# Sharing out the gate tiles anew among the convolution groups and the last head of attention

## The chip, the cores and the metric

The kernel runs on one core of a Trainium2 chip. TensorE (PE in the profile) does matrix products and transpositions, VectorE (DVE) and ScalarE (ACT) do the elementwise work, SyncE (SP) issues the transfers. The metric is the time of one execution in microseconds (us). All work is in fp32; PE takes it in the form fp32r, and each product is made of three (high by high, high by low, low by high part).

## What is computed

Two layers over 512 latent tokens and 256 context tokens with 1024 channels each. A layer does this, cut to what matters here:

```
proj = a @ w_in                        # a: modulated, normalised input
q, k, v -> differential attention of 4 heads
proj[P0:H0] -> pooling of 4 groups
proj[H0:G0] -> short convolution; z = x1 * longconv(v); y = x2 * longconv(z)
g = sigmoid(proj[:, G0:])              # 3 x 1024 gate columns
merged = g0 * attention + g1 * pooling + g2 * convolution
h = h + merged @ w_out ;  then a gated feed-forward layer
```

In layer 0 everything is done for latent and context tokens (768 columns), in layer 1 the context only gives keys and values, so that most products there have 512 columns.

## The kernel before

**Units.** A column tile of 128 outputs of `w_in` is a unit (`units`, L257 on): one load of 512 KB into `wr` (L268), the split into `wh` by ACT (L252) and `wl` by DVE (L253), 24 pairs of matmuls (layer 0: 512 and 256 columns each, 48 matmuls; layer 1: 24 of 512) into an accumulator tile `d` in PSUM (L285), and an eviction. There are two accumulators `d` in layer 0 and three in layer 1.

**Gate units.** 24 units for each layer give the gates (`gates`, `gate`). Their eviction is one sigmoid on ACT (L935) into a tile `gt`, and a store to DRAM (`gsp`, L936), from where the merge reads it back later. Nothing else waits for them.

**Convolution groups.** The 512 channels of the long convolution are taken in four groups of 128. A group begins with three units (`hyena_in`: v, x1, x2), whose eviction (`short`) is one ACT instruction (L895) and four of DVE (L899) in layer 0. Then come the steps of `stage`: F makes the filter's spectrum (L672 to L710), S transposes v and x1 (L839, L840) and transforms them, 1 is the spectral product on DVE (`spectral`, L791 to L795), M goes back and forward again (L863 on), 2 is the second product, Z the last transformation (L880, L881). The small letters f, s, q, m, w, z are the same steps for the context.

**The order.** `PROG` writes the order out by hand, one string for each layer; h is a unit of the next group, g takes the next gate unit off the list:

```
        if what == "g":
            gates.pop(0)()
            norm_more(2)
            return
...
            dense += units(win, 8, [12 + h], a, rng, pool)
            dense += qkv_units(h + 1) if h + 1 < HEADS else gates
```

The letters are priorities, no more: the framework's scheduler fixes each engine's order when the kernel is built, and lets an engine take a later letter's instruction where its own cost model says that the earlier one is not ready. On the chip each engine then works its list in order.

**Attention.** The first head's three units (v, k, q) follow the string's first part. Then for each of the four heads `HEAD` orders scores (L1053, L1054), exponentials (L1066, L1070), transpositions (L1094) and values (L1109); each f in it takes one unit off `dense` (`fill`): the head's pooling unit (`pool`) and the next head's three. The last head has no next head, and its list is the pooling unit and whatever is left of `gates`. Within attention the tile `gt` comes from the pool `pp` of five buffers, all of which one pooling unit uses.

Of the kernel before, what the change touches and what calls it, by code (L numbers as in the profile page):

```python
# [36 lines left out]
NCOL = 129  # L37
FFN_PARTS = ((6, 5, 5, 6), (8, 7, 7))

PROG = ('FggS1ggMfs2gggZgqmFwhhhSz1gMfs2ggZqmFwhhhSz1ggMfs2ggggZggqmFwhhhSz1gMfs2gggZgqm wz',  # L40
        'FgS1gggMFhhhS2ggZgg1gMFhhhS2ggZgg1ggMFhhh2ggSZg1ggggM 2gZ')
HEAD = ("01rfrA23fcrVfBrfU", "01rfrfrA23fVcfBrfU")


# [100 lines left out]
def build(ctx: ExitStack, tc: tile.TileContext, io: dict, out: bass.AP, dbg=None):  # L145
# [763 lines left out]
    def layer(l, a, hs, first, prepare):  # L909
# [73 lines left out]

        early, late = PROG[l].split()
        for what in early:
# [540 lines left out]
```

## Time and profile before

| | |
|---|---|
| median of 3 runs | 2394.58 us (2389.93 to 2403.16) |
| profiled execution, its own time | 2393.87 us |
| its span, first to last instruction | 2392.1 us |
| PE busy | 2325.6 us (97%) |
| DVE busy | 1722.3 us (72%) |
| ACT busy | 983.6 us (41%) |
| mean granted clock of PE | 0.991 |

Busy time is the union of an engine's instructions. The ends of matmuls are modelled, so PE counts as busy in stretches where it has little room as well as where it has none. The clock is a share of 2.4 GHz; it is granted at 1.00 or at 0.50 (1.2 GHz), and what stands between is a mean over the window.

### The profile page before, as it was taken

What the parts mean: (1) busy time and instruction counts of PE and PEld (TensorE: products, weight loads), DVE (VectorE), ACT (ScalarE), POOL (GpSimd) and SP (SyncE); (2) the same over time, 40 slices, a digit from 0 to 9 for tenths busy, and PEclk for the clock granted to TensorE, in tenths of its full rate; (3) what the DMA queues carried; (4) which work ended last, traced back from release to release, by engine and by line L of the source; (5) the groups of instructions that cost most, each with busy time, mean ns of one, the idle gap of its engine ahead of it and who ended that gap; (6) DMA issues with size and microseconds to landing.
All of it is one profiled execution on the core that took longest, in us unless ns stands there. A gap on an engine that the chain in (4) does not pass through costs nothing. (4 is left out here: it accounts for less than half of the span.)

```text
span 2392.1 us, 33306 instructions
## 1 busy us (share of the span) xinstructions
PE 2325.6 (97%) x12834; PEld 1981.7 (83%) x12834; DVE 1722.3 (72%) x3135; ACT 983.6 (41%) x1657; POOL 2.7 (0%) x8
## 2 busy tenths in 40 slices
PE   6999899999999999999999999999999999999998
PEld 3888688888878878888888888888888789888888
DVE  5688877999888785666768726899888778333336
ACT  6433334367762352121133424433377635312223
POOL 0000000000000000000000000000000000000000
PEclk9999899999989999999999999999999999999999
DMA  7222132321137543444725525344311444332324
GB/s 265 71 96 81 44 103 71 124 95 67 45 133 253 185 156 130 130 146 158 232 88 170 167 98 162 125 165 162 119 56 46 168 152 154 113 97 95 96 92 150
DMA packets 117801, 302.47 MB, mean 126 GB/s; under 512 B 13445, under 2 KB 27397, under 8 KB 116618
## 3 DMA queue, kind: packets, MB, share of 16 engines
q1 hardware_dynamic: 117642, 300.34, 37.9%
q8 instruction: 101, 1.65, 0.3%
q14 instruction: 58, 0.48, 0.1%
HBM read 266.74 MB, written 33.55 MB: 126 GB/s over the span
## 5 line engine op out<-in xcount | busy, mean ns | idle before, releaser
L252 ACT CAST wh<-wr 128x1024 fp32r<-128x1024 f32 (+3 forms) x327 | 331.0, 1013 | 933.2 <-PE d L285 756.1
L285 PE MATMUL d<-ah,wh 128*128 128x512 f32 (+1 forms) x2320 | 707.4, 354 | 6.8 <-ACT si L1371 2.8
L285 PE MATMUL d<-al,wh 128*128 128x512 f32 (+1 forms) x2320 | 709.9, 354 | 0.1
L285 PE MATMUL d<-ah,wl 128*128 128x512 f32 (+1 forms) x2320 | 706.6, 353 | 2.1 <-DVE wl L253 2.0
L253 DVE TENSOR_TENSOR wl<-wr,wh 128x1024 fp32r<-128x1024 f32 (+3 forms) x327 | 383.5, 1173 | 163.4 <-ACT wh L252 153.5
L285 PEld LDWEIGHTS d<-ah,wh 128*128 128x128 f32 x2320 | 387.8, 188 | 71.7 <-ACT si L1371 3.2
L285 PEld LDWEIGHTS d<-ah,wl 128*128 128x128 f32 x2320 | 388.8, 188 | 64.1 <-DVE wl L253 3.0
L285 PEld LDWEIGHTS d<-al,wh 128*128 128x128 f32 x2320 | 389.0, 188 | 61.5 <-DVE al L350 0.8
L489 DVE SCALAR_TENSOR_TENSOR junk<-mr,cb 128x512 bf16<-128x512 f32 x256 | 176.4, 689 | 13.4 <-DMA mr<-in_w_mod_rows_dram 8.2
L285 PE MATMUL d<-hh,wh 128*128 128x512 f32 (+1 forms) x584 | 179.1, 341 | 3.4 <-DVE h L1406 3.4
L285 PE MATMUL d<-hh,wl 128*128 128x512 f32 (+1 forms) x584 | 178.9, 341 | 0.0
L285 PE MATMUL d<-hl,wh 128*128 128x512 f32 (+1 forms) x584 | 178.7, 341 | 0.0
L1380 DVE TENSOR_TENSOR si<-d,si 128x512 f32<-128x512 f32 (+2 forms) x48 | 36.9, 768 | 174.3 <-PE d L285 174.3
L285 PE MATMUL d<-xs,wh 128*128 128x512 f32 x576 | 145.0, 358 | 0.8 <-ACT mx L1183 0.6
L1406 DVE SCALAR_TENSOR_TENSOR h<-d,mod,h 128x512 f32<-128x512 f32 (+1 forms) x96 | 58.5, 615 | 83.3 <-PE d L285 83.0
L285 PEld LDWEIGHTS d<-hh,wh 128*128 128x128 f32 x584 | 102.4, 190 | 17.9 <-issue 3.8
L285 PEld LDWEIGHTS d<-hl,wh 128*128 128x128 f32 x584 | 102.2, 190 | 13.6
L285 PEld LDWEIGHTS d<-hh,wl 128*128 128x128 f32 x584 | 102.4, 190 | 13.1
L285 PEld LDWEIGHTS d<-xs,wh 128*128 128x128 f32 x576 | 94.7, 189 | 18.1 <-ACT mx L1183 0.9
L285 PE MATMUL d<-xs,wl 128*128 128x512 f32 (+1 forms) x288 | 87.7, 358 | 0.0
L795 DVE TENSOR_TENSOR Y<-Y,T 128x1024 f32<-128x1024 f32 (+1 forms) x80 | 84.7, 1059 | 0.2
L794 DVE TENSOR_TENSOR T<-U,K 128x1024 f32<-128x1024 f32 (+1 forms) x80 | 83.1, 1059 | 0.0
(294 smaller groups left out, 3207.8 us busy)
## 6 DMA issues: line engine op xcount, KB each, us to landing
wr<-in_w_in_dram SPq DMA_DIRECT2D x104, 512.0 KB, 3.4
wr<-in_w_ffn_in_dram SPq DMA_DIRECT2D x96, 512.0 KB, 3.3
mr<-in_w_mod_rows_dram SPq DMA_DIRECT2D x160, 256.0 KB, 3.6
wr<-in_w_out_dram SPq DMA_DIRECT2D x32, 512.0 KB, 3.3
ksp<-K SPq DMA_DIRECT2D x28, 384.0 KB, 2.8
K<-ksp SPq DMA_DIRECT2D x8, 1344.0 KB, 7.7
wr<-in_w_ffn_out_dram SPq DMA_DIRECT2D x24, 448.0 KB, 3.4
gsp<-gt SPq DMA_DIRECT2D x24, 384.0 KB, 2.5
```

What stands on the lines that cost most here:

```text
L252: A.copy(hi, src)
L253: V.tensor_tensor(out=lo, in0=src, in1=hi.bitcast(F32), op=ALU.subtract)
L285: PE.matmul(o, w[:, c0:c0 + P], x[k][xi][:, c:c + nn], start=(k == 0 and pi == 0), stop=(k == K - 1 and pi == 2))
L489: V.scalar_tensor_tensor(out=junk[:], in0=raw[hf], scalar=1.0, in1=cb[v][hf][:, 0:512], op0=ALU.mult, op1=ALU.mult, accum_out=pv[:, v, hf, ...
L794: V.tensor_tensor(out=t[:], in0=ub, in1=kb, op=ALU.mult)
L795: V.tensor_tensor(out=y[:], in0=y[:], in1=t[:], op=ALU.add)
L1380: V.tensor_tensor(out=sg[f][:, cs], in0=o, in1=sg[f][:, cs], op=ALU.mult)
L1406: V.scalar_tensor_tensor(out=hs[d][:, cs], in0=o, scalar=mods[l][:, 40 + d, s:s + 1], in1=hs[d][:, cs], op0=ALU.mult, op1=ALU.add)
```

## The change

```diff
-PROG = ('FggS1ggMfs2gggZgqmFwhhhSz1gMfs2ggZqmFwhhhSz1ggMfs2ggggZggqmFwhhhSz1gMfs2gggZgqm wz',
-        'FgS1gggMFhhhS2ggZgg1gMFhhhS2ggZgg1ggMFhhh2ggSZg1ggggM 2gZ')
+PROG = ('FggS1gMfs2ggZgqmFwhhhSz1ggMfs2gggZqmFwhhhSz1ggMfs2ggZgqmFwhhhSz1gMfs2gggZgqm wz',
+        'FgS1gggMFhhhS2ggZgg1gMFhhhS2ggZgg1ggMFhhh2ggSZg1ggM 2gZ')
```

In layer 0 the four groups held 8, 3, 8 and 5 letters g and hold 6, 5, 5 and 5; 24 become 21, and the three gate units left over go to the last head of attention, which had none. In layer 1 the last group loses two of the four g between its first product and M; 23 become 21, and the last head gets three gate units in place of one. The number of units, their order in the list of gates and every instruction in them stay the same.

## Rows read from the trace of the kernel before

**Rows 1.** DMA issues of the page: a gate tile's store (KB, us to landing).

```profile
gsp<-gt SPq DMA_DIRECT2D x24, 384.0 KB, 2.5
```

**Rows 2.** Windows of 10 us: PE, PEld, DVE, ACT, POOL busy, clock, DMA share, GB/s.

```profile
250.00:260.00 10.00, 5.14 (x22) 4.31 (x21) 9.54 (x14) 3.25 (x5) 0.00 (x0) 0.83 0.17 52
260.00:270.00 10.00, 2.98 (x15) 2.16 (x14) 9.84 (x14) 2.47 (x7) 0.00 (x0) 0.66 0.12 39
270.00:280.00 10.00, 10.00 (x57) 9.12 (x57) 7.46 (x14) 1.18 (x3) 0.00 (x0) 0.83 0.01 2
...
660.00:670.00 10.00, 7.88 (x44) 6.31 (x43) 7.83 (x17) 6.74 (x16) 0.00 (x0) 0.97 0.09 16
670.00:680.00 10.00, 7.20 (x23) 4.73 (x23) 9.61 (x22) 6.63 (x17) 0.00 (x0) 0.50 0.21 77
680.00:690.00 10.00, 10.00 (x52) 8.59 (x51) 6.87 (x16) 6.34 (x14) 0.00 (x0) 0.85 0.00 0
...
1870.00:1880.00 10.00, 7.19 (x42) 5.68 (x41) 8.92 (x22) 8.61 (x18) 0.00 (x0) 1.00 0.31 105
```

**Rows 3.** Windows cut where a group's first latent transposition (L839) starts; then attention.

```profile
106.07:209.03 102.96, 102.96 (x594) 88.99 (x593) 86.86 (x120) 40.88 (x66) 0.00 (x0) 1.00 0.24 80
209.03:309.05 100.02, 88.14 (x485) 75.78 (x484) 83.47 (x118) 35.65 (x59) 0.00 (x0) 0.93 0.20 68
309.05:412.99 103.94, 103.94 (x606) 90.32 (x605) 86.09 (x120) 39.45 (x64) 0.00 (x0) 1.00 0.27 91
...
500.90:551.00 50.10, 47.97 (x291) 41.07 (x289) 48.77 (x136) 35.01 (x84) 0.00 (x0) 1.00 0.28 95
551.00:605.15 54.15, 54.15 (x341) 47.53 (x341) 48.68 (x127) 38.51 (x91) 0.00 (x0) 1.00 0.21 70
```

**Rows 4.** Timeline of ACT, layer 0: evictions of gate and convolution units (start, us).

```profile
163.48 0.80 ACT L935 ACTIVATE gt<-d 128x768 f32<-128x768 f32 x1
...
207.32 0.81 ACT L935 ACTIVATE gt<-d 128x768 f32<-128x768 f32 x1
...
221.33 0.80 ACT L935 ACTIVATE gt<-d 128x768 f32<-128x768 f32 x1
...
229.65 0.80 ACT L935 ACTIVATE gt<-d 128x768 f32<-128x768 f32 x1
...
251.97 0.99 ACT L895 ACTIVATE fm<-d,cols 128x768 f32<-128x768 f32 x1
...
363.16 0.80 ACT L935 ACTIVATE gt<-d 128x768 f32<-128x768 f32 x1
```

**Rows 5.** Timeline of DVE, layer 0: ends of second products, evictions of convolution units.

```profile
166.76 1.22 DVE L795 TENSOR_TENSOR Y<-Y,T 128x1024 f32<-128x1024 f32 x1
...
241.44 1.79 DVE L899 SCALAR_TENSOR_TENSOR fm<-d,cols,fm 128x511 f32<-128x511 f32 x3
...
268.02 1.22 DVE L795 TENSOR_TENSOR Y<-Y,T 128x1024 f32<-128x1024 f32 x1
...
270.96 0.48 DVE L899 SCALAR_TENSOR_TENSOR fm<-d,cols,fm 128x255 f32<-128x255 f32 x1
```

**Rows 6.** Timeline of PE, second group: the hole's end and the next unit.

```profile
269.39 3.75 PE L880 MATMUL yo<-idft,Y 128*128 128x128 f32 x16 [5.29 <-DVE Y L795]
272.80 0.90 PE L285 MATMUL d<-ah,wh 128*128 128x512 f32 x2
```

**Rows 7.** Groups of DVE by line, window 209 to 309.

```profile
L253 DVE TENSOR_TENSOR wl<-wr,wh 128x1024 fp32r<-128x1024 f32 x7 | 8.6, 1223 | 1.8 <-ACT wh L252 1.8
```

**Rows 8.** Windows: convolution stage of layer 1, in which DVE hardly pauses.

```profile
1520.00:1730.00 210.00, 209.78 (x982) 171.91 (x981) 194.79 (x274) 70.57 (x98) 1.04 (x2) 1.00 0.43 145
```

**Rows 9.** Timeline of ACT, last head of layer 1: table loads around its gate unit.

```profile
1879.88 1.28 ACT L935 ACT_TABLE_LOAD   x1
1881.17 0.60 ACT L935 ACTIVATE gt<-d 128x512 f32<-128x512 f32 x1
...
1883.35 1.28 ACT L1066 ACT_TABLE_LOAD   x1
```

## The prediction, made before the changed kernel ran

> **What bounds the kernel now.** I read the page first: PE is busy for 97% of the span, so the time is PE's work plus what PE loses. The change adds and removes no instruction that computes; it can only move these losses. So I looked for them in windows of 10 us. Outside the start and the merges there are three in the stretches that the change touches [rows 2]. (a) Layer 0, second convolution group, 250 to 280: PE is idle for 4.86 and 7.02 us and the granted clock falls to 0.83, 0.66 and 0.83. Weighted with the busy time of each window the clock costs 5.14 x 0.17 + 2.98 x 0.34 + 10 x 0.17 = 3.6 us; with the 11.9 us idle the loss is 15.5. (b) Layer 0, last head, 660 to 690: 2.12 + 2.80 = 4.9 us idle and, in the same way, 0.2 + 3.6 + 1.5 = 5.3 us by the clock (half speed, 1.2 GHz, for the whole second window): 10.2. (c) Layer 1, last head: 2.8 us idle at full clock. Together 28.5 us: what the change could win if it filled all three and opened nothing.
>
> Next, whether PE is the only bound of the groups. Cut at the first transposition of each, the first three groups take 102.96, 100.02 and 103.94 us [rows 3]. The second has 109 and 121 matmuls fewer than its neighbours; a unit has 48, so it holds 2.3 and 2.5 units less, 19 and 21 us of PE work at the 8.3 us from one gate's eviction to the next (221.33 to 229.65, [rows 4]). Yet it is only 2.9 and 3.9 us shorter; the rest of its PE time became hole (a). So a group takes about 100 us whatever PE is given: a chain through DVE (first product, M, second product, context, filter), with DVE busy for 83 to 87 us of each.
>
> The hole's cause is in DVE's list [rows 5]. The unit that PE finished first came while DVE was pausing in M, and three of its four DVE evictions ran at 241.44. The fourth, and all of the next unit's (its ACT part ran at 251.97, [rows 4]), stood behind the second product: they follow from 270.96, after the product's last instruction ended at 269.24. Both accumulators `d` were then taken, so the third unit of the trio began at 272.80 [rows 6], 3.6 us after the product, and PE ran dry in between. A gate unit has no DVE eviction and doesn't block in that way. The letters give only the order in which units are drawn: one gate was evicted at 207.32 [rows 4], before S of its group, though its letter stands after S.
>
> **The change part by part.**
>
> *First group, 8 to 6 letters.* Six units end between its S and 163.48; all six were gates. Now the last two are units h, whose evictions meet the second product (it ends at 167.98, [rows 5]). By the 3.6 us above, the third h starts at 171.5: 8.0 us without a unit, less 1.9 us of the 16 transformations L880 (3.75 us at half clock, [rows 6]), times 1.3 for the clock as in (a): a new loss of 8.
>
> *Second and third group, 5 letters each.* About two gates are drawn ahead of S, three stay behind it, and the first two h are the fourth and fifth unit. The fifth ends 54.1 us after S (363.16 less 309.05), the second product 61.9 us after it (167.98 less 106.07), the third h starts at 65.5: 11.4 us, less 1.9 and about 0.7 for other transformations, times 1.3: 12 each.
>
> So PE would lose 8 + 12 + 12 = 32 in place of 15.5, and has 1.4 units less to do before the fourth group's S (18 gates done by then in place of about 19.4): 16.5 less 11.6 is +4.9. By the chain the three groups take 100.0 each and 1.22 us [rows 7] for every `wl` above the second group's seven, 101.5 with 8 to 8.5 units: 304.5 against 306.9, that is -2.4. The floor is three times 100.0, -6.9. I take -2.4, since it rests on a whole measured group, and keep -6.9 and +4.9.
>
> *Fourth group to the last head, layer 0.* Some 1.6 gates fewer, 13.3 us. DVE is full in the first head (48.77 of 50.10), PE in the second (54.15 of 54.15, DVE 48.68) [rows 3]. If DVE's fullness swallows it, only 1.6 `wl` are saved, -2.0; if PE carries its lead in the two accumulators into the heads where DVE has room, -13.3. Two units of lead fit and DVE has 5 us of room in each of two heads, so I take two thirds, -9.
>
> *Last head, layer 0.* Three gates, 3 x 8.3 = 24.9, against loss (b), 10.2, which they should fill: +14.7. Their stores are 384 KB each and land 2.5 us after issue [rows 1], their weights 512 KB, beside a DMA share of 0.21 at most there [rows 2]; hidden. The first `gt` must wait for a buffer of `pp` that the pooling unit holds; while it waits, one accumulator is taken and the next gate has the other, so this shifts the fill by some us and costs nothing more while a second unit covers it; without that cover the loss (b) would stay, +10.
>
> *Layer 1.* Two gates are 2 x 5.5 = 11.0 us (an estimate: two thirds of the columns of layer 0, two thirds of 8.3). Before the last head PE is busy for 209.78 of 210 us and DVE for 194.79 [rows 8]: between two `wl` (-2.4) and all of it (-11.0), by the same reasoning and with three accumulators, I take -7. In the last head +11.0 against loss (c), 2.8: +8.2. Each g also advances the context's normalisation, which is done in the first few letters, so nothing changes there.
>
> Sum: -2.4 - 9 + 14.7 - 7 + 8.2 = +4.5. On the profiled execution's own 2393.87 (1.8 more than its span, 0.7 below the median) that gives 2398. With all lower ends 2386, with all upper ends (+4.9 - 2.0 + 14.7 - 2.4 + 8.2 = +23.4) 2417.
>
> **The rivals.**
>
> *No new hole: faster.* The planner might place the h units so that their evictions fall into M or behind the product, as it did at 241.44, or put gates there. Then the three losses go and nothing comes: -28.5, 2365. For it: DVE is idle for 16 to 18 us in each group [rows 3], and the DVE part of an h eviction needs 1.79 and 0.48, about 2.3 [rows 5]. Against it: the 100 us of the second group, and that the letters leave the first three groups with fewer gates behind S than the six that covered the second product in the first group. It decides itself at the second unit after the fourth gate: if its DVE part runs before the product ends, there is no hole.
>
> *DVE holds the time: slower.* PE's lead behind the fourth group and in layer 1 is lost, because every evicted tile waits for DVE or for the memory of the convolution stage. Then -2.4 - 2.0 + 14.7 - 2.4 + 8.2 = +16, 2410. It decides where the first head's scores start: if not earlier than the `wl` saved, this is the case.
>
> *Tables.* The gate's sigmoid stands alone in layer 1's last head and brings one table load ahead of it and one for the exponentials behind it, 1.28 us each [rows 9]. Three gates in layer 0 bring up to six, two more in layer 1 up to four: 12.8 us of ACT, which is busy for 8.61 of 10 us in layer 1's window and 6.7 at most in layer 0's [rows 2]. If exponentials are what the last heads wait for, it adds to the sum: +17, 2411. If the gates are evicted together, or ACT has room, it is nothing. The Trainium skill (ScalarE: Activation LUTs, "What ACT_TABLE_LOAD costs" and "Table sets: the hidden batching unit") asks to do all work of one table set before switching, which speaks against this edit, and prices a switch at 1.28 us and 1.38 us of drain; with its 2.66 the ten would be 26.6. The trace agrees with the 1.28 and shows no drain around it: the load starts at 1879.88 and the sigmoid at 1881.17.
>
> **How the numbers follow.** No difference that can be told is within 0.5%, 12 us. My forecast has 0.48, no new hole 0.25, DVE 0.15, tables 0.12. The forecast's own range, 2386 to 2417, lies mostly within 12 us: 0.35 of its 0.48 same, 0.11 slower, 0.02 faster. No new hole is faster but for a trace (0.25). DVE (+16) gives 0.10 slower and 0.05 same, tables (+17) 0.08 and 0.04. Faster 0.27, same 0.44, slower 0.29. The range reaches down to 2364, which leaves out half of the faster case (0.12), and up to 2418, beyond which I see 0.06.
>
> **What would show it.** Windows of 10 us: 250 to 280 full at clock 1.00 and, in place of that hole, PE idle for 5 to 9 us some 55 to 65 us behind each S, each with a fall of the clock. Group lengths of 101 to 102. In the last head of layer 0 no window below 9 us busy and the clock at 1.00. Evictions L899 at the end of the second product rather than ahead of it. If the groups are full and about 95 us long, the floor of 100 was wrong, and so is the prediction; if they are 103 again, the planner drew more units ahead than I think. If the exponentials in the last heads come later by more than their table loads, it is the tables.

## The result, and the profile after

The changed kernel takes 2436.73 us (median of 6 runs, 2431.81 to 2440.28), the kernel before 2396.06 on the same chip (6 runs, 2389.93 to 2403.16): ratio 1.0168, interval 1.0147 to 1.0190. It is 40.7 us slower, and outside the range of the prediction, which ended at 2418. The profiled execution has a span of 2435.8 us, 43.7 more than before.

The page of the changed kernel, its span and its busy time by engine:

```profile
span 2435.8 us, 33313 instructions
PE 2338.4 (96%) x12834; PEld 1993.4 (82%) x12834; DVE 1723.6 (71%) x3135; ACT 987.2 (41%) x1661; POOL 2.7 (0%) x8
```

DVE and ACT have the work they had, 1722.3 and 983.6 us before; PE is 12.8 us longer busy, with the same instructions. So of the 43.7 us, 12.8 are matmuls that take longer and 30.9 are time in which PE does nothing. The windows below cut the changed kernel at the marks of the prediction. In order: the three groups (start of L839 to start of L839), the fourth group to the first scores (L1053), the first three heads, the last head of layer 0 up to its last norm (L313), the feed-forward and the start of layer 1, layer 1's groups up to its first scores, its first three heads, its last head.

```profile
105.28:210.56 105.28, 97.46 (x534) 84.07 (x533) 84.51 (x118) 37.48 (x62) 0.00 (x0) 0.94 0.21 69
210.56:315.20 104.64, 95.40 (x533) 82.50 (x532) 84.90 (x119) 37.35 (x62) 0.00 (x0) 0.95 0.22 73
315.20:419.85 104.65, 95.47 (x534) 82.49 (x533) 85.01 (x119) 37.39 (x62) 0.00 (x0) 0.95 0.22 74
419.85:509.61 89.76, 80.83 (x458) 69.63 (x456) 81.50 (x120) 35.35 (x62) 1.47 (x2) 0.96 0.28 91
509.61:671.96 162.35, 155.93 (x959) 135.90 (x957) 138.21 (x355) 112.81 (x265) 0.00 (x0) 0.99 0.20 66
671.96:760.67 88.71, 86.30 (x528) 75.55 (x528) 68.37 (x158) 53.22 (x102) 0.00 (x0) 1.00 0.52 177
760.67:1538.18 777.51, 766.63 (x4308) 663.57 (x4306) 526.33 (x1053) 242.37 (x328) 0.00 (x0) 0.99 0.48 155
1538.18:1758.67 220.49, 210.58 (x983) 171.62 (x981) 203.89 (x294) 77.09 (x113) 1.04 (x2) 0.98 0.40 138
1758.67:1892.95 134.28, 134.11 (x774) 115.93 (x774) 109.92 (x250) 95.22 (x215) 0.00 (x0) 0.98 0.17 56
1892.95:1957.18 64.23, 61.39 (x304) 51.17 (x303) 42.72 (x90) 40.03 (x79) 0.00 (x0) 0.95 0.50 172
```

The same windows of the kernel before, from the fourth group on (its first three are [rows 3]):

```profile
412.99:500.88 87.89, 87.83 (x517) 76.61 (x516) 79.45 (x112) 37.30 (x64) 1.47 (x2) 1.00 0.32 103
500.88:658.33 157.45, 154.70 (x962) 134.88 (x960) 141.78 (x367) 113.64 (x267) 0.00 (x0) 1.00 0.20 68
658.33:730.80 72.47, 67.28 (x382) 57.15 (x383) 60.57 (x147) 43.25 (x92) 0.00 (x0) 0.91 0.48 166
...
1508.03:1732.07 224.04, 223.42 (x1045) 182.97 (x1043) 207.39 (x297) 80.24 (x117) 1.04 (x2) 1.00 0.43 145
1732.07:1861.06 128.99, 128.70 (x758) 111.09 (x759) 109.74 (x249) 95.53 (x215) 0.00 (x0) 1.00 0.16 55
1861.06:1913.08 52.02, 48.56 (x256) 39.78 (x255) 39.69 (x88) 35.75 (x74) 0.00 (x0) 1.00 0.53 182
```

Subtracted stretch by stretch, against the terms of the prediction:

| stretch | predicted | measured |
|---|---|---|
| three groups, layer 0 | -2.4 (-6.9 to +4.9) | +7.6 |
| fourth group and heads 0 to 2, layer 0 | -9 (-13.3 to -2.0) | +1.9 + 4.9 = +6.8 |
| last head, layer 0 | +14.7 | +16.2 |
| groups and heads 0 to 2, layer 1 | -7 (-11 to -2.4) | -3.6 + 5.3 = +1.7 |
| last head, layer 1 | +8.2 | +12.2 |
| all else (start, feed-forward, end) | 0 | -0.9 |
| sum | +4.5 | +43.6 (spans: 43.7) |

The last heads cost about what was said. What was to pay for them was not there: the stretches that gave up gate units became longer, not shorter.

Windows of 10 us of the changed kernel, in the columns of [rows 2], show why. A hole stands in each of the three groups (the third's, at 372, like the second's), in front of the first scores, and in front of those of layer 1:

```profile
160.00:170.00 10.00, 4.71 (x24) 4.20 (x24) 10.00 (x12) 2.53 (x5) 0.00 (x0) 0.83 0.28 92
170.00:180.00 10.00, 7.49 (x27) 6.33 (x26) 7.12 (x14) 1.02 (x2) 0.00 (x0) 0.50 0.00 0
270.00:280.00 10.00, 5.45 (x24) 4.89 (x25) 9.66 (x16) 0.62 (x1) 0.00 (x0) 0.67 0.27 87
490.00:500.00 10.00, 3.23 (x17) 2.80 (x18) 9.78 (x22) 4.17 (x10) 0.00 (x0) 0.88 0.32 106
...
1750.00:1760.00 10.00, 3.93 (x16) 2.92 (x15) 9.81 (x17) 6.47 (x11) 0.00 (x0) 0.52 0.12 40
```

But for 170 to 180, DVE is busy for 9.7 to 10 us in each window of a hole. The last head of layer 0 runs at clock 1.00, as was forecast, but one of its windows is below 9 us (690 to 700, PE busy for 7.6).

The hole of [rows 2] at 250 to 280 was in the main two pauses. The first, in which PE waited for DVE's part of the filter, is gone after the change. The second, 5.29 us ahead of L880 [rows 6], is still there in the second group (5.42 us), and now stands in the first and third group too. The first pause, before the change:

```profile
256.14 0.76 PE L694 MATMUL fc<-ones,fa 128*128 128x1 f32 x4 [4.86 <-DVE fa L691]
```

In the first group of the changed kernel, the timeline of ACT, then that of PE and DVE (start, us, then the idle time before and its releaser):

```profile
162.70 0.98 ACT L895 ACTIVATE fm<-d,cols 128x768 f32<-128x768 f32 x1
...
167.35 3.75 PE L880 MATMUL yo<-idft,Y 128*128 128x128 f32 x16 [5.29 <-DVE Y L795]
173.19 0.58 PE L863 MATMUL zo<-yh,idfth 128*128 128x256 f32 x1 [2.09 <-ACT yh L252]
...
168.93 0.74 DVE L899 SCALAR_TENSOR_TENSOR fm<-d,cols,fm 128x511 f32<-128x511 f32 x1
172.41 1.13 DVE L899 SCALAR_TENSOR_TENSOR fm<-d,cols,fm 128x255 f32<-128x255 f32 x2
```

This is the hole that the prediction named, near its size: two convolution units done, their DVE evictions behind the second product, both accumulators held, PE idle for 5.29 + 2.09 us (L880 is at the head of PE's list; 5.42 + 2.09 in the second and third group). Then the clock is at half, 1.2 GHz, and L880 takes 3.75 us where the first group of before, without a hole, took 1.95:

```profile
168.56 1.95 PE L880 MATMUL yo<-idft,Y 128*128 128x128 f32 x16
```

The three groups were run with the changed string in three further kernels of those below: layer 0 alone, 6, 5, 5 and 8 letters, and no table loads. In all four traces each engine works the same instructions in the same order through these groups, but the half clock fell on different stretches. In the first group the clock is 0.94, 0.95, 0.97 and 0.97, and the group takes 105.3, 104.1, 103.8 and 103.7 us; in the second, where it is 0.95 in the changed kernel and 0.94 in the others, 104.6 there and 105.6 to 105.9 in them. PE's idle time in the first group is the same, 7.8 to 8.1 us; its busy time is not (97.5 to 95.7). So the half clock lengthens a group without any change of order. The first and second group with 6, 5, 5 and 8 letters:

```profile
107.12:210.90 103.78, 95.72 (x533) 82.78 (x532) 84.52 (x118) 37.46 (x62) 0.00 (x0) 0.97 0.21 70
210.90:316.80 105.90, 96.83 (x534) 83.64 (x533) 84.92 (x119) 37.44 (x62) 0.00 (x0) 0.94 0.21 72
```

The sums of the three groups lie closer together, at 314.4 to 315.1 us in the four traces, and at 306.7 to 306.9 in three traces with the string of before. Differences of sums are therefore read below rather than those of single groups.

### The profile page after: what moved, and what is told of

Read it like the earlier page. It is cut to its first block, busy times and chain, and to the rows that moved or that the text cites. A ratio compares the mean times of both kernels' runs of the same rounds, so it can differ in the third digit from the quotient of the medians.

```text
span 2435.8 us, 33313 instructions
## 1 busy us (share of the span) xinstructions
PE 2338.4 (96%) x12834; PEld 1993.4 (82%) x12834; DVE 1723.6 (71%) x3135; ACT 987.2 (41%) x1661; POOL 2.7 (0%) x8
## 4 chain that ended last, share of the span: by engine, by line
PE 83%; DVE 10%; ACT 3%; issue 2%; DMA 1%; SPq 0%; DVEq 0%; ACTq 0%
PE d L285 70%; DVE wl L253 2%; PE av L1109 1%; PE s L1053 1%; PE dx L285 1%; ACT wh L252 1%; PE yo L880 1%; PE sc L1054 1%; PE fg L672 1%; DVE junk L489 1%; DVE Y L812 1%; DVE T L810 1%; PE zo L863 1%; PE at L1094 1%; DMA dec<-in_dec_dram 1%
## 5 line engine op out<-in xcount | busy, mean ns | idle before, releaser
L285 PE MATMUL d<-ah,wh 128*128 128x512 f32 (+1 forms) x2320 | 714.6, 357 | 13.4 <-DVE k L1016 5.1
L285 PEld LDWEIGHTS d<-ah,wh 128*128 128x128 f32 x2320 | 392.7, 190 | 79.3 <-DVE k L1016 5.3
L489 DVE SCALAR_TENSOR_TENSOR junk<-mr,cb 128x512 bf16<-128x512 f32 x256 | 176.4, 689 | 16.1 <-DMA mr<-in_w_mod_rows_dram 8.5
```

Source lines behind the costliest of these rows:

```text
L285: PE.matmul(o, w[:, c0:c0 + P], x[k][xi][:, c:c + nn], start=(k == 0 and pi == 0), stop=(k == K - 1 and pi == 2))
L489: V.scalar_tensor_tensor(out=junk[:], in0=raw[hf], scalar=1.0, in1=cb[v][hf][:, 0:512], op0=ALU.mult, op1=ALU.mult, accum_out=pv[:, v, hf, ...
```

## The experiments

Each ratio is to the kernel before on the same chip, whose median is 2395 to 2397 us; the lengths of stretches come from one profiled execution of each kernel. "The string of layer 0" is the first string of the diff, changed or as before.

**Each layer alone.** The changed string for one layer, the string of before for the other.

> The changed order in layer 0 alone (6, 5, 5, 5 and three gates in the last head); layer 1 as before. The trace of the changed kernel has layer 0 about 30 us behind at the start of layer 1. If each part costs what it shows there, this kernel takes 28 to 31 us more than before, a ratio of 1.012. If a good part of it comes from the planner laying out the whole program differently, the ratio is another one, and the rest of the loss shows up with layer 1 alone.

> The changed order in layer 1 alone (two gates fewer in the last group, three in the last head); layer 0 as before. If each part costs what the changed kernel's trace shows, 12 to 15 us more than before, a ratio of 1.0055, all of it behind the last group's first product: PE idle for some 10 us ahead of the first scores and the last head 12 us longer. My prediction had +1 us for it.

Layer 0 alone: 2428.09 us, ratio 1.0129 (1.0104 to 1.0153), +31, as expected. Layer 1 alone: 2405.80, 1.0046 (1.0028 to 1.0064), +8.7, less than the 12 to 15 expected. Together, 39.7, they nearly give the change. For layer 1 alone the three stretches are 220.24, 133.51 and 61.64 us: what was won ahead of the scores (3.8) is lost in the heads (4.5), and the last head's +9.6 is the whole result.

**Is it the last head, or the sharing out?** Layer 0 with 6, 5, 5 and 8 letters, none left for the last head, layer 1 as before:

```diff
-PROG = ('FggS1gMfs2ggZgqmFwhhhSz1ggMfs2gggZqmFwhhhSz1ggMfs2ggZgqmFwhhhSz1gMfs2gggZgqm wz',
+PROG = ('FggS1gMfs2ggZgqmFwhhhSz1ggMfs2gggZqmFwhhhSz1ggMfs2ggZgqmFwhhhSz1gMfs2ggggggZgqm wz',
```

> Layer 0 with 6, 5, 5 and 8 letters, none left for the last head; layer 1 as before. The holes in the first three groups stay. If the last head is a bad place by itself (table loads, its buffers), its 16 us go and the three gates fill the hole ahead of the first scores: about +8 to +10 us against before, 2404. If no place takes gate units for nothing (a chain through DVE in the groups, PE in the heads), the fourth group grows by what the last head gives back less that hole: +18 to +22 us, 2414.

2421.16 us, 1.0101 (1.0077 to 1.0124): +24, and beyond both numbers. All 24 gate units are within the groups, as before, and still the kernel is slower. The three groups take 314.6 us, as in the changed kernel; the three units cost 100.32 - 89.76 = 10.6 us in the fourth group. The last head (72.4) is as before. Heads 0 to 2 take 165.0 us, 7.6 more than before, and no run settles why. The first three groups hold 84 matmuls fewer than before and are 7.7 us longer, wherever the units that leave them go: what was taken out there bought nothing.

**The evictions of the convolution units first.** The changed kernel, with the priority of `short` in layer 0 raised, so that its ACT and DVE parts go ahead of the products.

```diff
+            with tc.high_priority(offset=ahead[0] if l == 0 else 0):
                 for o, c0, nn in acc.pieces():
                     A.activation(y[:, c0:c0 + nn], o, AF.Identity, ...)
...
                         V.scalar_tensor_tensor(out=y[:, c0 + a0:c0 + nn - b0], ...)
```

> The changed kernel, but in layer 0 the evictions of the convolution units (ACT and the four DVE instructions) have the priority that the weight splits have, so that they don't stand behind the second product. If these evictions make the holes, the three holes of 5.3 us and more behind the second products go. If PE's loss there is what costs time, the kernel gains up to 37 us (the three holes with their clock), about 2400. If the group's length is a chain through DVE of about 100 us, the groups go from 105 to 101 to 102 and only 10 to 13 us come back, about 2425.

2466.15 us, 1.0285 (1.0258 to 1.0312): both expectations missed. The holes of the first two groups are gone (PE idle for 1.4 us and for none), but PE draws its units early: these groups hold 643 and 663 matmuls and take 113.2 and 113.7 us. The third takes 115.0 with 15.0 of idle time, and in the fourth PE has nothing left. Windows of that kernel:

```profile
106.60:219.80 113.20, 111.79 (x643) 96.61 (x642) 88.09 (x121) 42.26 (x67) 0.00 (x0) 1.00 0.25 82
...
460.00:470.00 10.00, 0.00 (x0) 0.00 (x0) 9.97 (x10) 0.00 (x0) 0.00 (x0) 0.50 0.00 0
```

It changes too much at once to price the holes; it shows that units drawn early fill a group and are missing later.

**Other counts, none left for the last head** (layer 1 as before): 7, 6, 6 and 5 letters, and 7, 7, 7 and 3.

```diff
-PROG = ('FggS1gMfs2ggZgqmFwhhhSz1ggMfs2gggZqmFwhhhSz1ggMfs2ggZgqmFwhhhSz1gMfs2gggZgqm wz',
+PROG = ('FggS1ggMfs2ggZgqmFwhhhSz1ggMfs2gggZgqmFwhhhSz1ggMfs2gggZgqmFwhhhSz1gMfs2gggZgqm wz',
...
+PROG = ('FggS1ggMfs2ggZgqmFwhhhSz1ggMfs2ggggZgqmFwhhhSz1ggMfs2ggggZgqmFwhhhSz1gMfs2gZgqm wz',
```

> The kernel before with the same 24 letters g in layer 0 shared out as 7, 6, 6 and 5, none left for the last head; layer 1 as before. By the rule that the traces give so far (a hole opens when the second h unit behind S is finished ahead of the second product's end, 62 us after S; four gate units behind S are too few, six are enough), five gates behind S make a sixth unit end at 63 us and leave holes of 0 to 3 us in each group. If holes are what costs, the 15.5 us of the second group go, 2381. If the group is a chain through DVE of 100 us, the three groups fall from 307 to 302 at most: -2 to -6 us, 2392.

> The same with 7, 7, 7 and 3. The first three groups as with 7, 6, 6, 5 or fuller, but the fourth has two gates fewer ahead of the first scores, and its DVE is full until then. By the chain, that stretch keeps its length and the PE time of two gates is lost there: +5 to +12 us against before. If PE can run ahead into attention in this stretch, as I took it for two thirds in the prediction, nothing is lost and the result is that of 7, 6, 6, 5.

2408.26 us (1.0044, 1.0030 to 1.0058) and 2403.31 (1.0028, 1.0016 to 1.0040). The first misses both numbers; the second is at +7.5, within its +5 to +12, and its fourth group nearly keeps its length (89.7 us against 87.9) with 420 matmuls in place of 517, as the expectation by the chain said. With 7, 6, 6 the idle time shrinks to 2.5 to 2.8 us a group, yet the groups take 105.2, 103.8 and 102.8. With 7, 7, 7 the second and third have no idle time, 102.0 and 104.2. No group of the two kernels is shorter than 102.0, with PE idle in it or not.

**Fewer letters for the second group, as before for the others**: 8, 2, 8 and 5 with one unit left, 8, 1, 8 and 5 with two left. The diff is against the kernel before.

```diff
-PROG = ('FggS1ggMfs2gggZgqmFwhhhSz1gMfs2ggZqmFwhhhSz1ggMfs2ggggZggqmFwhhhSz1gMfs2gggZgqm wz',
+PROG = ('FggS1ggMfs2gggZgqmFwhhhSz1gMfs2gZqmFwhhhSz1ggMfs2ggggZggqmFwhhhSz1gMfs2gggZgqm wz',
...
+PROG = ('FggS1ggMfs2gggZgqmFwhhhSz1gMfs2ZqmFwhhhSz1ggMfs2ggggZggqmFwhhhSz1gMfs2gggZgqm wz',
```

> The kernel before with one gate fewer in the second group of layer 0, where its one hole is (8, 2, 8, 5), and that gate in the last head; layer 1 as before. If the group's length is the chain's, the gate leaves the group at no gain or at one weight split, 1.2 us, and costs 8.3 us in the last head less what it fills of the 10.2 us lost there: -3 to +1 us, 2394. If spreading the gates was right and only the hole is wrong, taking from the group with the hole widens it and costs 8 us more: 2404.

> The same with two gates taken from the second group (8, 1, 8, 5) and two in the last head. By the chain, the second of them finds the last head's loss already filled and costs its full 8 us there, less a split: +3 to +8 us against before, 2402. If the first gate's room is not what the last head lacks, both cost alike.

2411.46 us (1.0068, 1.0055 to 1.0081) and 2418.92 (1.0095, 1.0081 to 1.0109); both worse than either theory. The edit did not do to the second group what it was made for: the group holds 581 and 515 matmuls where it held 485, since units that come later in the list were drawn into it, and takes 104.2 and 103.3 us. The matmuls are missing in the third group (522 and 540 in place of 606), which takes 104.2 and 104.9 us, no less than before. So these runs say nothing of a second group with less work; the last heads show what a unit costs there. The second group and the last head of the first kernel, then of the other:

```profile
208.60:312.80 104.20, 100.77 (x581) 86.79 (x580) 86.13 (x120) 38.90 (x63) 0.00 (x0) 1.00 0.25 83
669.82:747.08 77.26, 73.13 (x433) 64.03 (x432) 64.58 (x155) 48.36 (x97) 0.00 (x0) 0.96 0.49 167
```

```profile
208.70:312.00 103.30, 92.11 (x515) 78.66 (x514) 83.58 (x118) 35.77 (x60) 0.00 (x0) 0.95 0.22 74
669.87:752.90 83.03, 78.63 (x480) 68.14 (x479) 65.77 (x156) 51.75 (x100) 0.00 (x0) 1.00 0.51 172
```

With none, one, two and three gate units the last head of layer 0 takes 72.5, 77.3, 83.0 and 88.7 us: 4.8, 5.7 and 5.7 for each. Even the first, with loss (b) to fill, is not free.

**Idle units.** The string of layer 0 changed, with five more letters j in the first three groups: each loads the first gate's weights again, runs a whole unit and evicts it to a tile that nothing reads. 41 us more work for PE, five loads and five DVE splits.

```diff
-PROG = ('FggS1gMfs2ggZgqmFwhhhSz1ggMfs2gggZqmFwhhhSz1ggMfs2ggZgqmFwhhhSz1gMfs2gggZgqm wz',
+PROG = ('FggS1gjMfs2ggjZgqmFwhhhSz1ggMfs2gggjZjqmFwhhhSz1ggMfs2ggjjZgqmFwhhhSz1gMfs2gggZgqm wz',
...
+            if what == "j":
+                units(win, 8, [28], a, rng, spill)[0]()
+                return
```

> Layer 0 changed as in the change, layer 1 as before, and five further units in the groups' steps (two, two and one... in all 5 in the first three groups) that compute a gate tile once more and throw it away: 41 us of additional work for PE and five weight splits for DVE, of no use for the output. If a group is a chain whose own transformations on PE run at half clock when PE has been idle, the additional units close the holes, the groups fall from 105 back to 102 to 104 and the kernel is 0 to 8 us faster than layer 0 changed alone (2428). If PE's work sets the length, it is slower by what the holes cannot hold, 4 us and more.

2421.47 us, 1.0110 (1.0092 to 1.0127): 6.6 us less than without the extra work (2428.09), 4.6 less by the ratios, as was expected. The two intervals overlap, so the sum of the groups has to say it. The three groups and the stretch to the scores:

```profile
106.98:209.71 102.73, 102.73 (x594) 89.02 (x592) 86.76 (x120) 40.74 (x66) 0.00 (x0) 1.00 0.21 73
209.71:313.99 104.28, 104.28 (x606) 90.58 (x605) 86.16 (x120) 38.91 (x64) 0.00 (x0) 1.00 0.24 84
313.99:417.73 103.74, 103.74 (x603) 90.08 (x602) 84.19 (x116) 40.25 (x65) 0.00 (x0) 1.00 0.24 79
417.73:509.20 91.47, 91.47 (x542) 79.90 (x540) 82.95 (x118) 37.76 (x65) 1.47 (x2) 1.00 0.31 105
```

No idle time, the clock at 1.00 throughout, 310.75 us for the three groups against 315.06 in the kernel without the idle units. The change had taken 1.75 units of work out of these groups; putting five in made them shorter, not longer.

**Idle units in layer 1.** Layer 1 alone changed, with two letters j (11 us of PE work) where the two g were.

> Layer 1 changed, layer 0 as before, and in the place of the two gates taken out of the last group two units that compute a gate tile once more and throw it away: 11 us of additional PE work. If the last group and the way to the first scores is a chain through DVE that PE's room doesn't shorten, and the hole there only cools PE, this kernel takes as long as layer 1 changed alone (2406), -3 to +3 us. If PE's work sets the time there, it is up to 11 us slower, 2417.

2405.56 us, 1.0048 (1.0033 to 1.0064), against 2405.80 without them. The room that the two units left in layer 1 is worth nothing. Its heads 0 to 2:

```profile
1729.38:1858.35 128.97, 128.70 (x758) 111.03 (x759) 109.75 (x249) 95.32 (x215) 0.00 (x0) 1.00 0.16 55
```

They are back at the 129.0 of before, at clock 1.00; the last head takes 61.6, with the idle units (61.58) as without (61.64).

**No table loads in the last heads.** The changed kernel with a plain copy in place of the sigmoid of those gate units (three tiles of each layer go without their sigmoid).

```diff
-                A.activation(g[:, c0:c0 + nn], o, AF.Sigmoid)
+                A.activation(g[:, c0:c0 + nn], o, AF.Copy if "pp" in tg else AF.Sigmoid)
```

> The changed kernel, but the gate units in the last heads are evicted by a plain copy: the sigmoid is left out there (three tiles of each layer), and with it the table loads. If table loads lengthen the last heads, up to 12 us come back, 2425. The last head of layer 0 measured +16.2 where I had +14.7 without tables, that of layer 1 +12.3 where I had +8.2: by that at most 1.5 and 4 us are left for them, 2431 to 2436.

2440.72 us, 1.0182 (1.0168 to 1.0196), not below the 2436.73 of the changed kernel. Its last heads:

```profile
679.55:768.29 88.74, 86.83 (x528) 75.53 (x528) 68.49 (x158) 48.75 (x99) 0.00 (x0) 1.00 0.52 177
1899.58:1962.26 62.68, 59.84 (x305) 50.28 (x304) 42.59 (x90) 37.33 (x77) 0.00 (x0) 0.97 0.50 176
```

In layer 0 the same 88.7 us, in layer 1 1.6 less. Tables cost at most that, and perhaps nothing: with layer 1 alone changed, its last head takes 61.64 us with all its tables. Nor are there ten more of them: the changed kernel has 37 table loads, the kernel before 33, this one 32.

**Idle matmuls in the holes.** To take the half clock away and as little else as possible: the string of layer 0 changed, and behind the second convolution unit of each group 40 matmuls of 256 columns into the unused quarter of its accumulator.

```diff
+                if ps["layer"] == 0 and ms[0] == fill:
+                    for _ in range(40):
+                        PE.matmul(accs[0].pad, ws[0][0][:, 0:P], x[0][0][:, 0:256], start=True, stop=True)
```

> Layer 0 with the changed string, layer 1 as before (as in the run with layer 0 alone, 2428.1 us), and behind the second convolution unit of each of the three groups 40 further matmuls of 256 columns into the unused quarter of its accumulator, whose result nothing reads: some 4.7 us of TensorE work a group, put into the hole of 5.3 us ahead of the 16 transformations L880, with no load, split or eviction. If the half clock behind the hole lengthens the chain's own steps (theory): the records show the clock at 1.00 behind the second product (the 2.1 us of idle time between L880 and L863 may still lower it for one row), L880 is shorter, the groups take 102.5 to 104 us in place of 104 to 106, and the time is 2420 to 2424. If the order of the evictions alone is what the five added units mended (rival), the groups stay at 104 to 106 and the time at 2428, 3 us up or down. If TensorE's work bounds the groups, 14 us more work makes it up to 14 us slower: 2442.

2424.39 us, 1.0107 (1.0091 to 1.0124), against 1.0129 (1.0104 to 1.0153) without them: just above the 2420 to 2424 expected, but the intervals overlap, so the profile has to say it. PE in the first group, then the windows of the three groups:

```profile
165.55 4.95 PE L290 MATMUL d<-ah,wh 128*128 128x256 f32 x40
170.33 1.95 PE L884 MATMUL yo<-idft,Y 128*128 128x128 f32 x16
176.72 0.38 PE L867 MATMUL zo<-yh,idfth 128*128 128x256 f32 x1 [4.44 <-ACT yh L253]
```

```profile
108.95:211.69 102.74, 97.72 (x566) 84.79 (x565) 84.44 (x118) 37.39 (x62) 0.00 (x0) 0.98 0.21 71
211.69:317.07 105.38, 100.74 (x582) 87.87 (x580) 85.06 (x119) 37.75 (x62) 0.00 (x0) 0.97 0.21 73
317.07:419.39 102.32, 97.52 (x566) 84.88 (x565) 84.91 (x119) 37.39 (x62) 0.00 (x0) 0.97 0.22 75
```

The transformations (L884 here) are back at 1.95 us, and the first and third group lose 1.3 and 2.9 us against layer 0 alone; the second, with 105.4 against 105.8, hardly changes. The sum falls by 4.6 us, to 310.4, more than the 0.7 by which the sums of the same instructions differ. The hole behind the transformations grows from 2.09 to 4.44 us, as DVE is still at its evictions and splits: part of what the clock gives is waited away. One thing changed beside the clock: the scheduler moved a split of weights (`wl`, 1.2 us of DVE) from within the second product to behind it.

**The stores on another queue.** In the changed kernel DVE waits for the loads of `dec` (L674); before, it never did there. Groups of waits of DVE, 105 to 420 us (total, times, longest), then SP's and DVE's timeline behind one store:

```profile
DVE g L676 <- DMA dec<-in_dec_dram: 6.8, 4, 2.9
```

```profile
304.79 0.33 SPq L936 DMA_DIRECT2D gsp<-gt  x1
305.22 0.37 SPq L674 DMA_DIRECT2D dec<-in_dec_dram  x1
...
309.63 0.69 DVE L676 TENSOR_TENSOR g<-fg,dec 128x512 f32<-128x512 f32 x1 [2.90 <-DMA dec<-in_dec_dram]
```

The gate's store stands on SP's queue ahead of the load and waits for the gate's eviction, which ends at 304.8. So the stores were given to ScalarE's queue: in the kernel with layer 0 changed, in that with the idle matmuls, and in the kernel before.

```diff
-            SP.dma_start(out=gsp[mt - 28, :, 0:W], in_=g[:, 0:W])
+            A.dma_start(out=gsp[mt - 28, :, 0:W], in_=g[:, 0:W])
```

> The changed string in layer 0 alone (2428.1 us), with the stores of the gate tiles (L936) issued by ScalarE behind the eviction instead of by SyncE. If the loads of dec behind these stores lengthen the groups (theory): VectorE no longer waits for dec, the second group is some 3 us shorter, each other 1 us, and the time falls by 4 to 6 us to 2422 to 2424, with the holes and the half clock still there. If the wait for dec only takes the place of another (rival): within 2 us of 2428.

> The idle matmuls in the three holes (2424.4 us) and the stores on the other queue together. If half clock and the waits for dec are the two causes, both gains add: the three groups fall to 100 to 102 us each and the time to 2416 to 2420. If either hides behind the other: 2422 to 2425.

> The kernel before with the stores of the gate tiles issued by ScalarE. No load of dec waits in it before 520 us, so by the theory it stays within 3 us of 2396; if ScalarE's queue is better or worse for another reason, both layers would show it here.

2437.22 us (1.0183, 1.0169 to 1.0197), 2432.05 (1.0152, 1.0138 to 1.0166) and 2409.66 (1.0061, 1.0049 to 1.0074): all three missed, each 8 to 14 us slower than its kernel with the stores on SP. The third shows that the other queue costs this by itself, from the fourth group on and in layer 1; why was not followed up. So only the first three groups can be read. There the wait for `dec` is gone (0.3 us in all), and the three groups take 313.5 us instead of 315.1, and 310.9 instead of 310.4 with the matmuls in the holes. The wait was real (6.8 us in all), but most of it stood in place of another.

## Why the prediction was wrong

**The last heads: right in kind.** Layer 0: three gates of 8.3, less the loss filled: PE is busy for 19.0 us more in that stretch, at clock 1.00 in place of 0.91, and idle for 2.8 less: +16.2 against +14.7. Layer 1: +12.2 against +8.2. There, with layer 1 alone changed, it is +9.6; in the full change the stretch also has the clock at 0.95, which the term did not foresee.

**The tables: rightly a rival with a small chance.** Up to ten loads were priced at 12.8 us; the change brings four (37 in place of 33), 5.1 us of ACT at 1.28 each. Without them layer 1's last head is 1.6 us shorter and layer 0's not at all. The Trainium skill (ScalarE: Activation LUTs, "What ACT_TABLE_LOAD costs") adds a drain of 1.38 us to each switch; this trace does not agree, since in the changed kernel a load starts at 695.06, 0.02 us behind the instruction before it, and the sigmoid at 696.35, as the load ends.

**The holes in the groups: right in place, too small, and given the wrong weight.** The third unit was to start late behind the second product, with PE idle for 6.1, 8.8 and 8.8 us, and a loss of 8, 12 and 12 with the clock. PE is idle for 7.8, 9.2 and 9.2, and with the clock (by its mean, 0.06, 0.05 and 0.05 of the busy time, which is a little too much, since PE is idle in part of the half clock) loses some 13.7, 14.0 and 14.0. The step that failed is the one after it: "I take -2.4, since it rests on a whole measured group". The 100 us of the second group of before were read as a floor set by a chain through DVE, to which each split adds 1.22 us. Only kernels with the string of before repeat it: a second group with nearly as few matmuls, 515 against 485, took 103.3 us, and those of 522 to 607 took 102.0 to 105.9 in no order of their work (the run with the evictions first apart). The account that the prediction kept only as its upper bound, PE's work and what PE loses, was the better one:

- Idle time of PE in the three groups: 11.9 us before [rows 3], 26.2 after: +14.3.
- 84 matmuls fewer (1685 to 1601), 1.75 units of 8.3 us: -14.5. But busy time falls only from 295.0 to 288.3, by 6.7. The 7.8 between the two is about what half clock costs: by the mean clock of the rows it takes 15.4 us of the busy time after and 6.2 before.
- +14.3 - 14.5 + 7.8 = +7.6.

The upper bound had this sum at +4.9. So PE's work that moves out is eaten by the holes, and the half clock behind them lengthens the steps that the group waits for. That it does so is shown by the traces in which the order is the same and the clock alone differs. How much of the 8.1 us that layer 0 alone loses in the three groups is half clock is less sharp: idle matmuls give back 4.6 and whole idle units 4.3, both with the clock up, but the first also moved a split on DVE, and the second also lets the convolution units end after the second product.

What is left in these two runs, 3.5 and 3.8 us, lies in the second group alone (105.4 and 104.3 against 100.0); the first and third are as before or shorter. With idle units the second group has 606 matmuls where it had 485, and no idle time, so PE's work is its length. With idle matmuls PE is still idle there for 4.6 us, and the cause is open: evictions that now stand behind the second product are a likely one, but the run that moved them changed too much. The waits for `dec` account for about 1.6 us by the run that took them away, and for nothing in the one with idle matmuls.

**The lead that was to be carried: this term does not exist.** "[I]f PE carries its lead in the two accumulators into the heads where DVE has room" was taken at two thirds, -9 and -7; measured +6.8 and +1.7. This was the largest miss, 24.5 of the 39.1 us below. PE had no lead: behind the fourth group its next unit waits for DVE, which is at rows of the modulation (L489) and at k.

```profile
498.40 1.01 PE L285 MATMUL d<-ah,wh 128*128 128x512 f32 x2 [5.11 <-DVE k L1016]
```

Fewer units there make PE idle: 8.9 us in place of 0.1 from the fourth group to the scores, 9.9 in place of 0.6 in layer 1. The heads behind become longer. In layer 0 the first head takes 54.1 us against 50.1; the clock is 0.97 in it, but 3.9 us are a wait for DVE's split of v:

```profile
555.48 0.43 PE L1109 MATMUL av<-ath,vt 128*128 128x256 f32 x1 [3.91 <-DVE vt L253]
```

Half clock is at most a part of the +4.9 of these heads: in the kernel with the idle units the clock is 1.00 up to the scores and through the heads, and they still take 160.2 us, against 157.5 before and 162.4 after the change. Why DVE comes later there was not tested. These heads with the idle units:

```profile
509.20:669.35 160.15, 155.70 (x961) 134.69 (x959) 140.67 (x364) 112.98 (x266) 0.00 (x0) 1.00 0.20 67
```

In layer 1 heads 0 to 2 take 134.3 us against 129.0, with the clock at 0.98 and with 16 matmuls more (774 against 758). With two idle units in layer 1 the heads are back at 129.0 and the time does not change: the units that were taken out had cost nothing where they were. The rival "DVE holds the time" (+16) had the mechanism and its mark: the scores come no earlier than the splits saved. But it too took a small gain there, -2.0 and -2.4, where both stretches became longer.

In sum: 10.0 us in the groups, 15.8 and 8.7 in the two terms of lead, 1.5 and 4.0 in the last heads, -0.9 elsewhere, 39.1 in all between +4.5 and +43.6.

## What to carry to other kernels

Where a chain through another engine sets the pace, work on TensorE beside it can be free, and taking it out can make the chain slower: here half clock followed the idle time, and the chain's own 16 transformations took 3.75 us in place of 1.95. Before work is moved out of a stretch, price the stretch by PE's idle time and granted clock after the move, not by a floor read from one group of one kernel; and count the work at its full price where it goes, unless a run shows that the place has room. A run with idle units put back costs little and tells whether the work that left was free.

## What the hardware showed that was not expected

- 41 us of matmuls more, spread over three groups, made these groups 4.3 us shorter (315.06 to 310.75) and the kernel no slower (2428.09 to 2421.47, the intervals overlap).
- The same instructions in the same order took 103.7 to 105.3 us in the first group, by where the half clock fell.
- PE's idle times of 4.9 to 5.4 us in the groups, before and after the change, are followed by half clock of 3.4 to 13.7 us. The same three short pauses in the last head of layer 1 (0.9, 0.5 and 1.4 us) are followed by full clock before and by 6.8 us of half clock in the changed kernel, so the same pauses did not cost the same in two kernels.
- Moving 48 stores of gate tiles from SyncE's queue to ScalarE's cost 14 us (2395.33 to 2409.66), though ScalarE is busy for 41% of the span.
